# Feed-forward products of layers 0 to 2 by rows of tokens, five of their sixteen units by Strassen's scheme, and a written ScalarE order in stick-breaking attention

## The chip, the cores and the metric

One Trainium2 chip, one core, one launch. The metric is the device time of the program in microseconds (us). Engines are called as in the profile: PE (TensorE, matrix products), PEld (its weight loads), DVE (VectorE), ACT (ScalarE), POOL (GpSimd), SP (SyncE, which issues most DMAs).

## What is computed

A trunk of four layers over 256 tokens of 1024 features, all in float32. Layer i has a mixer (0 and 3 retention, 1 convolution, 2 stick-breaking attention), then a squared-ReLU feed-forward part:

```python
for i in range(DEPTH):                       # DEPTH = 4
    h = rms_norm(x, norm_mix[i])
    x = x + mixer_i(h)                       # retention, conv, stick-breaking, retention
    x = x + squared_relu_mlp(rms_norm(x, norm_ffn[i]), ffn_w1[i], ffn_w2[i])
return rms_norm(x, final_norm)

def squared_relu_mlp(xn, w1, w2):            # w1 1024 x 4096, w2 4096 x 1024
    h = jax.nn.relu(xn @ w1)
    return (h * h) @ w2
```

The stick-breaking mixer takes logits z of queries and keys, masks them, forms log-sigmoids and their running sums along the keys, exponentiates, and multiplies with the values; 16 heads of 64.

## The kernel before

**Number format.** Each float32 operand is cut in two: a rounded part hi (a cast on ACT) and the rest lo (a subtraction on DVE), and a product is hi·hi + hi·lo + lo·hi. For weights these are `wh` (L361, ACT, 128x1024) and `wl` (L368, DVE, 128x1024), written into five buffers each (pool `wp`), one pair for each unit of 128x1024 weights. Weights come as `raw` tiles of two units by DMA from SP.

**Layout.** x is kept with features on the partitions: four tiles of 128x512 (p = 0 to 3, each two blocks of 128 features by 256 tokens). The next mixer or feed-forward part takes `z`, eight tiles (z0 to z7, two for each x tile): hi by ACT (L475), lo by DVE (L476). `norm_sq` squares x (L486, ACT) and adds up over the tiles on POOL (L491); the sum over features then is a matmul with a column of constants (L436).

**The feed-forward part** (`ffn`, from L640). The first product makes 16 pairs of blocks of h (units p = 0 to 15, `pair_w`): each step is one matmul of 256 columns (lo of the weight, L558) and one of 512 (hi of the weight with hi and lo of z side by side, L562). `sum_w` adds the two halves (L605 ACT, L606 DVE), then ReLU, square, and the split into hi and lo (L411, L412): 32 tiles h of the pool `big`, two for each unit. In layers 0 to 2 the second product goes the same way with h in the place of z: four pairs (p = 0 to 3) over eight units of 512 rows, the weight as stationary operand. Where the last pair would leave the next mixer waiting, it is made of three matmuls of 256 columns a step (L542 to L544): all of p = 3 in layer 0, the last two of its eight units in layers 1 and 2. The squared norm factor, spread over the partitions (`norm_rb`), is multiplied in at the end (L704), the result is added to x (L705), and `norm_pair` makes z for the next mixer.

**Layer 3 already works another way** (`final`, L708): tokens are on the output's partitions. Four accumulators C[t, c] (t = token half, c = half of the 1024 output features) begin with 16 transposes of x. The h blocks are stationary, the weights (512 columns) move. Eleven of the sixteen units of 256 rows are plain: 24 matmuls each. Five (`FAST` = 0, 1, 13, 14, 15) go by Strassen's scheme: seven block products instead of eight, 21 matmuls; `fast_unit` forms their weight combinations (four additions L384, five casts L391 and five subtractions L392 of 128x512, beside one L361 and one L368), and `ffn` the h combinations (L661 to L670). `MIXED` is the order in which plain and Strassen units alternate, `REST` the four plain units at the end, first for c = 0, then for c = 1. All matmuls of it have line L722.

**What sets the order.** PE, DVE, ACT, POOL and SP each run their own queue in order. Most of it is arranged by a scheduler at build time. In the convolution PE and DVE (in its second half ACT and POOL too) follow the program text; in the stick-breaking mixer PE does, by a string of steps (`SB_ORDER`): p = projection of a unit, n = norms of q and k of one block of four heads, u and t = transposes of q and k, l = logits and masks, s = the ACT and DVE chain abs, exp, ln, max, split (L1549 to L1555), w = running sums and exp (L1568), v = values, m = product with the values. PSUM has eight banks: four `acc`, four `mis`.

**POOL in layer 0.** The convolution's 18 strips (L1045, a product of 128x512) are formed ahead of the convolution, in buffers of the pool `big` (36 buffers, handed on in turn). A strip can be written when the former tenant of its buffer has been used for the last time.

Of the kernel before, what the change touches and what calls it, by code (L numbers as in the profile page):

```python
# [15 lines left out]
P = 128  # L16
# [17 lines left out]
    "p00 p01 r p02 p03 p10 n0 p11 p12 p13 u0 t0 p20 n1 l0 s0 p21 p22 w02 p23 n2 w00 u1 t1 p30 l1 p31 p32 s1"  # L34
    " w01 w12 p33 w10 u2 t2 w11 v00 n3 l2 s2 v01 v02 w22 v03 u3 t3 w20 v10 l3 v11 s3 w21 v12 w32 v13 w31 w30"
    " m0 m1",
    "m2 m3",
)

# [18 lines left out]
FAST = (0, 1, 13, 14, 15)  # L58
MIXED = (2, 0, 3, 4, 1, 5, 13, 6, 14, 7, 15, 8)
# [8 lines left out]
def _plan():  # L68
    u = []
    for i in range(DEPTH):  # L70
# [30 lines left out]
        if i + 1 < DEPTH:  # L101
            for p in range(4):
                u += _b_pair("ffn_w2", i, p * 256, 8)
        else:
            u += [("ffn_w2", i, "a", kb, c * 512) for kb in MIXED for c in range(2)]
            u += [("ffn_w2", i, "a", kb, c * 512) for c in range(2) for kb in REST]
# [139 lines left out]
class Trunk:  # L246
    def __init__(self, ctx, tc, xT, w, prm, cst, fin, gn, out):
# [16 lines left out]
        self.un = 0  # L264
        nc = self.nc
# [217 lines left out]
    def norm_sq(self, p):  # L483
        nc = self.nc
        q = self.tmp()
        nc.scalar.activation(out=q, in_=self.x[p], func=AF.Square)  # L486
        if self.sq is None:
            self.sq = q
        else:
            a = self.tmp()  # L490
            (nc.vector if p == 3 and self.quick else nc.gpsimd).tensor_add(a, self.sq, q)  # L491
            self.sq = a
# [18 lines left out]
    def norm_rb(self):  # L511
        nc = self.nc
        sq = self.sq[:, :S]
        nc.gpsimd.tensor_add(sq, sq, self.sq[:, S:])
        hl = self.split(sq)
        ps = self.mis()
        for e in range(2):
            nc.tensor.matmul(ps[:, :S], self.cr["m1"], hl[:, e * S : (e + 1) * S], start=e == 0, stop=e == 1)
        b = self.bc.tile([P, S], F32, name=self.nm("rb"), tag="rb")
        nc.vector.tensor_scalar(out=b, in0=ps[:, :S], scalar1=-1.0 / D, scalar2=EPS, op0=ALU.mult, op1=ALU.add)  # L520
        nc.vector.reciprocal(out=b, in_=b)
        return b

    def zs(self, k):
        return self.z[k]
# [55 lines left out]
    def pair_x(self, name, l, c0, acts, nkb, x, rb):  # L581
        nc = self.nc
        ps, pe = [self.acc(), self.acc()], self.mis()

        def onto(a):
            t = self.tmp()
            nc.vector.tensor_mul(v3(t, 2, S), v3(a, 2, S), self.b2(rb))
            nc.vector.tensor_add(x, x, t)

        for kb in range(nkb):  # L590
            w = self.unit((name, l, "b", kb, c0))
            if kb < nkb - 2:
                self.mm_w(ps, w, acts, kb * 4, kb == 0, kb == nkb - 3, keep=True)
            else:
                if kb == nkb - 2:
                    onto(self.sum_w(ps))
                self.mm_b(pe, w, acts, kb * 4, kb == nkb - 2, kb == nkb - 1)
        onto(pe)

# [27 lines left out]
    def res_pairs(self, name, l, acts, nkb, group, evac, before=None):  # L627
        for g in range(4 // group):
            ps = [self.acc() for _ in range(group)]
            for kb in range(nkb):  # L630
                if before is not None:
                    before(kb)
                for p in range(group):
                    w = self.unit((name, l, "b", kb, (g * group + p) * 256))
                    self.mm_b(ps[p], w, acts, kb * 4, kb == 0, kb == nkb - 1)
                    if kb == nkb - 1:
                        evac(g * group + p, ps[p])


    def ffn(self, i, nxt):  # L640
# [4 lines left out]
        def act(ps):  # L645
# [27 lines left out]

        def factor(k):
            if k == (2 if last else 0):
                rb.append(self.bcast(self.r, "rb", keep=True) if last else self.norm_rb())
                for x in held:
                    act(x)

        held = []  # L680
        for p in range(16):
            ps = self.pair_w(
                "ffn_w1", i, p * 256, self.zs, keep=p >= (3 if last else 4),
                before=factor if p == (3 if last else 2) else None,
# [5 lines left out]
            if last and p == 0:  # L690
                with self.tc.high_priority():
                    self.norm_r(False)

        acts = lambda k: h[k]
        if last:
            self.final(i, h, fast)
            return
        self.norm_begin()
        for p in range(4):
            pw = ("ffn_w2", i, p * 256, acts, 8)  # L700
            if p < 3 or i == 0:
                ps = self.pair_w(*pw, keep=True) if p < 3 else self.pair_b(*pw)
                t = self.tmp()
                nc.vector.tensor_mul(v3(t, 2, S), v3(ps, 2, S), self.b2(rb[0]))  # L704
                nc.vector.tensor_add(self.x[p], self.x[p], t)  # L705
            else:
                self.pair_x(*pw, self.x[p], rb[0])
            self.norm_pair(p, *nxt)  # L708


    def final(self, i, h, fast):
        nc = self.nc
        kw = dict(skip_group_check=True)
        self.table("sqrt_and_others")
# [950 lines left out]
```

## Time and profile before

| what | value |
|---|---|
| median of three runs | 1337.06 us (1336.6 to 1338.1) |
| the profiled execution's own time | 1338.49 us |
| its span, first to last instruction | 1336.7 us |
| second product of layer 3, 16 transposes included (L722) | 1244.7 to 1330.5 us |
| DVE, ACT, POOL busy | 1012.0, 806.8, 134.3 us |
| DMA | 244.56 MB, mean 183 GB/s |

The time outside the span is 1.8 us. How to read the views: a row of a group gives the line, engine, operation, tiles (out<-in, buffer numbers left out), shape and count, then busy time and mean of one. A timeline row gives start, duration and what it is; in square brackets the idle time of the engine before it and what ended it. Matmuls overlap: the time that one takes on PE is the step from its start to the next one's start, less than its own duration.

### The profile page before, as it was taken

How to read it: one execution, taken by the hardware profiler on the slowest of the kernel's cores; microseconds unless marked ns; L12 is line 12 of the kernel's file. 1: busy time of each engine (PE TensorE's matmuls, PEld its weight loads, DVE VectorE, ACT ScalarE, POOL GpSimd, SP SyncE). 2: the span in 40 equal slices, each digit the busy share in tenths (PEclk: the TensorE clock that was granted, in tenths of full speed). 3: DMA queues.
4: the chain of work that ended last, by engine and by line, in shares of the span. 5: the costliest groups of instructions: out<-in, count | busy, mean ns of one | idle time of the engine just before them, and what ended most of it. 6: DMA issues, size and time to landing. Idle time of an engine off the chain costs nothing.

```text
span 1336.7 us, 20778 instructions
## 1 busy us (share of the span) xinstructions
PE 1326.3 (99%) x8174; PEld 1160.2 (87%) x8174; DVE 1012.0 (76%) x1689; ACT 806.8 (60%) x1275; POOL 134.3 (10%) x123
## 2 busy tenths in 40 slices
PE   9999999999999999999999999999999999999998
PEld 8988888888999898888878898888888888888886
DVE  7977768875688688765688588755698776798985
ACT  7555556764456477744568677744565555577663
POOL 3200002000269110000100010000110000100000
PEclk9999999999999999999999999999999999999999
DMA  8545555555445645555453345555554554555552
GB/s 311 211 172 186 179 190 185 192 193 187 184 163 147 217 171 200 192 190 191 174 186 126 126 162 189 190 190 191 185 187 173 190 184 152 213 187 182 187 189 95
DMA packets 41731, 244.56 MB, mean 183 GB/s; under 512 B 4512, under 2 KB 9248, under 8 KB 14240
## 3 DMA queue, kind: packets, MB, share of 16 engines
q1 hardware_dynamic: 40768, 240.60, 50.4%
q10 hardware_dynamic: 864, 2.62, 0.6%
q8 instruction: 64, 1.05, 0.3%
q14 instruction: 35, 0.29, 0.1%
HBM read 241.27 MB, written 1.93 MB: 182 GB/s over the span
## 4 chain that ended last, share of the span: by engine, by line
PE 95%; POOL 1%; ACT 1%; DVE 1%; issue 1%; DMA 0%; POOLq 0%; DVEq 0%; ACTq 0%
PE acc L562 33%; PE acc L558 17%; PE acc L1024 6%; PE acc L1026 6%; PE acc L1025 6%; PE acc L722 5%; PE acc L542 3%; PE acc L544 3%; PE acc L543 3%; PE mis L562 2%; PE mis L558 1%; PE acc L1326 1%; POOL big L1122 1%; PE mis L722 1%; PE acc L1193 1%
## 5 line engine op out<-in xcount | busy, mean ns | idle before, releaser
L368 DVE TENSOR_TENSOR wl<-raw,wh 128x1024 fp32r<-128x1024 f32 (+1 forms) x435 | 539.4, 1245 | 206.5 <-ACT wh L361 200.8
L361 ACT CAST wh<-raw 128x1024 fp32r<-128x1024 f32 (+1 forms) x435 | 451.1, 1042 | 311.8 <-PE acc L562 153.5
L562 PE MATMUL acc<-z,wh 128*128 128x512 f32 x1152 | 399.4, 394 | 0.0
L558 PE MATMUL acc<-z,wl 128*128 128x256 f32 x1152 | 317.1, 280 | 0.9 <-DVE t L606 0.9
L562 PE MATMUL acc<-big,wh 128*128 128x512 f32 x800 | 277.5, 393 | 0.0
L562 PEld LDWEIGHTS acc<-z,wh 128*128 128x128 f32 x1152 | 214.3, 187 | 47.0
L558 PE MATMUL acc<-big,wl 128*128 128x256 f32 x800 | 221.4, 279 | 0.0
L558 PEld LDWEIGHTS acc<-z,wl 128*128 128x128 f32 x1152 | 216.5, 189 | 3.6 <-PE acc L562 1.1
L562 PEld LDWEIGHTS acc<-big,wh 128*128 128x128 f32 x800 | 149.4, 187 | 33.5
L558 PEld LDWEIGHTS acc<-big,wl 128*128 128x128 f32 x800 | 150.3, 189 | 0.7
L1024 PE MATMUL acc<-wh,z 128*128 128x512 f32 x352 | 137.9, 392 | 0.0
L1026 PE MATMUL acc<-wh,z 128*128 128x512 f32 x352 | 137.2, 390 | 0.0
L1025 PE MATMUL acc<-wl,z 128*128 128x512 f32 x352 | 137.2, 390 | 0.0
L491 POOL TENSOR_TENSOR t<-t,t 128x512 f32<-128x512 f32 x23 | 35.7, 1553 | 884.1 <-ACT t L486 814.6
L605 ACT COPY t<-acc 128x256 f32<-128x256 f32 x176 | 61.2, 371 | 100.2 <-PE acc L562 98.6
L606 DVE TENSOR_TENSOR t<-acc,t 128x256 f32<-128x256 f32 x176 | 68.3, 420 | 39.4 <-ACT t L605 39.0
L1026 PEld LDWEIGHTS acc<-wh,z 128*128 128x128 f32 x352 | 66.1, 188 | 14.7 <-issue 0.8
L1024 PEld LDWEIGHTS acc<-wh,z 128*128 128x128 f32 x352 | 66.1, 188 | 14.0 <-issue 0.8
L1025 PEld LDWEIGHTS acc<-wl,z 128*128 128x128 f32 x352 | 66.1, 188 | 13.2
L722 PE MATMUL acc<-wh,big 128*128 128x512 f32 x200 | 63.7, 390 | 0.0
L542 PE MATMUL acc<-z,wh 128*128 128x256 f32 x224 | 63.6, 284 | 0.0
L544 PE MATMUL acc<-z,wl 128*128 128x256 f32 x224 | 63.4, 283 | 0.0
(306 smaller groups left out, 1907.4 us busy)
## 6 DMA issues: line engine op xcount, KB each, us to landing
raw<-in_w SPq DMA_DIRECT2D x214, 1024.0 KB, 4.8
big<-in_gn SPq DMA_DIRECT2D x16, 256.0 KB, 5.3
raw<-in_w SPq DMA_DIRECT2D x7, 512.0 KB, 7.5
raw<-hd SPq DMA_DIRECT2D x8, 263.0 KB, 4.7
raw<-hd SPq DMA_DIRECT2D x8, 131.5 KB, 3.9
wh<-in_w ACTq DMA_DIRECT2D x2, 512.0 KB, 7.0
wl<-in_w ACTq DMA_DIRECT2D x2, 512.0 KB, 8.8
hd<-big SPq DMA_DIRECT2D x6, 143.5 KB, 2.1
```

The lines of the kernel that those rows point to most:

```text
L361: nc.scalar.copy(hi[:, s], src[:, s])
L368: self.nc.vector.tensor_sub(lo[:, s], src[:, s], hi[:, s])
L542: nc.tensor.matmul(o, wh[:, kk, cs], ah, start=st, stop=False, **kw)
L544: nc.tensor.matmul(o, wl[:, kk, cs], ah, start=False, stop=en, **kw)
L558: mm = nc.tensor.matmul(ps[m][:, :S], wl[:, kk, cs], a[:, :S], start=first and kk == 0, stop=False, **kw)
L562: nc.tensor.matmul(ps[m], wh[:, kk, cs], a, start=False, stop=last and kk == 3, **kw)
L605: nc.scalar.copy(o[:, s], ps[m][:, S:])
L606: nc.vector.tensor_add(o[:, s], ps[m][:, :S], o[:, s])
L722: self.tc.keep_in_program_order(nc.tensor.matmul(o, l, r, **k, **kw))
L1024: nc.tensor.matmul(ps[t], zh[:, s], wh[:, kk], start=k == 0, stop=False, skip_group_check=True)
L1025: nc.tensor.matmul(ps[t], zh[:, s], wl[:, kk], start=False, stop=False, skip_group_check=True)
L1026: nc.tensor.matmul(ps[t], zl[:, s], wh[:, kk], start=False, stop=k == 7, skip_group_check=True)
```

## The change

1. Layers 0 to 2 take the second product by rows of tokens as layer 3 does; the shared code is `down`, the two users are `middle` (layers 0 to 2) and `final`. `middle` starts C from zero, scales each C[t, c] by the token's factor while evacuating it (`scaled`, ACT; the last one half on ACT, half on DVE), transposes the result back (`turn`: 16 transposes a layer) and adds it to x from PSUM (`onto`). C[0, 0] and C[1, 0] are evacuated while the four last units of c = 1 run; C[0, 1] while the last twelve matmuls of C[1, 1] run; C[1, 1] after the last matmul. Its transposes, additions and z4 to z7 are a closure `rest` that the next mixer calls when it asks for z2.
2. `FAST` becomes (5, 6, 13, 14, 15) and `MIXED` (0, 5, 1, 2, 6, 3, 13, 4, 14, 7, 15, 8), for all layers. The split of h is done by DVE for p < 4 and by ACT for the others, in all layers (before: DVE in layers 0 to 2, ACT in layer 3).
3. The factor of layers 0 to 2 is a column for each token half (`norm_sums`, `norm_r2`) instead of a row over the partitions (`norm_rb`).
4. Stick-breaking: the masks are the first matmuls of a block's logits instead of the last; `s` is cut into its three parts, values are evacuated in a step `c` of their own; the unit's casts are called three units ahead (`SB_AHEAD`); ACT follows the program text, as PE did already.
5. Convolution: the fourth unit is fetched one step later, and the norm's column sums come in the third unit instead of the second.

The core of the diff:

```diff
 SB_ORDER = (
-    "p00 p01 r p02 p03 p10 n0 p11 p12 p13 u0 t0 p20 n1 l0 s0 p21 p22 w02 p23 n2 w00 u1 t1 p30 l1 p31 p32 s1"
+    "p00 p01 p02 r p03 p10 n0 p11 p12 p13 u0 t0 n1 p20 l0 s02 p21 s00 p22 s01 w02 p23 w00 u1 t1 n2 p30 l1 s12 p31 s10"
...
+SB_AHEAD = 3
-FAST = (0, 1, 13, 14, 15)
-MIXED = (2, 0, 3, 4, 1, 5, 13, 6, 14, 7, 15, 8)
+FAST = (5, 6, 13, 14, 15)
+MIXED = (0, 5, 1, 2, 6, 3, 13, 4, 14, 7, 15, 8)
...
+    def norm_r2(self, sums):
+        nc = self.nc
         ps = self.mis()
+        for t in range(2):
+            self.tc.keep_in_program_order(self.colsum(ps[:, t : t + 1], sums[:, t * P : (t + 1) * P], self.sc(1024)))
+        r2 = self.col(2, "r2")
+        nc.vector.tensor_scalar(out=r2, in0=ps[:, :2], scalar1=EPS, scalar2=None, op0=ALU.add)
+        nc.vector.reciprocal(out=r2, in_=r2)
+        return r2
 
     def zs(self, k):
+        if self.rest and k == 2:
+            rest, self.rest = self.rest, None
+            rest()
         return self.z[k]
...
-            how = "act" if last else "dve"
+            how = "dve" if p < 4 else "act"
             h.extend((self.split(s[:, :S], how), self.split(s[:, S:], how)))
-            if last and p in FAST:
+            if p in FAST:
...
+    def middle(self, i, h, fast, sums, nxt):
+        nc = self.nc
+        r2 = self.norm_r2(sums)
+        y, pt = {}, {}
+
+        def scaled(C, t, c, *cuts):
+            y[t, c] = self.tmp()
+            for s, on in cuts or ((slice(0, 512), "act"),):
+                if on == "act":
+                    nc.scalar.activation(out=y[t, c][:, s], in_=C[t, c][:, s], func=AF.Copy, scale=r2[:, t : t + 1])
+                else:
+                    nc.vector.tensor_scalar(
+                        out=y[t, c][:, s], in0=C[t, c][:, s], scalar1=r2[:, t : t + 1], scalar2=None, op0=ALU.mult
+                    )
+
+        def turn(t, c):
+            for q in range(4):
+                p = 2 * c + q // 2
+                if p not in pt:
+                    pt[p] = self.mis()
+                o = (q % 2) * S + t * P
+                self.tc.keep_in_program_order(
+                    nc.tensor.transpose(pt[p][:, o : o + P], y[t, c][:, q * P : (q + 1) * P], self.id)
+                )
...
+        def hook(C, at):
+            if at == 0:
+                for t in range(2):
+                    scaled(C, t, 0)
+                self.norm_begin()
+            if at == (REST[1], 0, 0):
+                for t in range(2):
+                    turn(t, 0)
+                for p in range(2):
+                    onto(p)
+                    self.norm_pair(p, *nxt)
+            if at == (REST[-2], 0, 1):
+                scaled(C, 0, 1)
+            if at == (REST[-1], 0, 1):
+                turn(0, 1)
+                for p in (2, 3):
+                    onto(p, 0)
+
+        C = self.down(i, h, fast, None, hook)
+        scaled(C, 1, 1, (slice(0, S), "act"), (slice(S, 512), "dve"))
+
+        def rest():
+            turn(1, 1)
+            for p in (2, 3):
+                onto(p, 1)
+                self.norm_pair(p, *nxt, False)
+            for p in (2, 3):
+                self.norm_sq(p, nc.vector)
+
+        self.rest = rest
...
-        with self.tc.manual_schedule(engines={mybir.EngineType.PE}):
+        with self.tc.manual_schedule(engines={mybir.EngineType.PE, mybir.EngineType.Activation}):
             go(SB_ORDER[0])
```

Two places of the build's order follow, and a third on POOL; in them the numbers tell buffers apart, and what stands in brackets is what an instruction waits for. First PE at the end of layer 0's second product. Before, its last rows (L542 to L544 on `big`) are followed by the convolution's first (on `z`):

```order
L542 MATMUL acc_3690<-big_3125,wh_3895 128x256
L543 MATMUL acc_3690<-big_3125,wh_3895 128x256
L544 MATMUL acc_3690<-big_3125,wl_3896 128x256
L542 MATMUL acc_4007<-z_3306,wh_3989 128x256 [waits Activation_49]
L543 MATMUL acc_4007<-z_3306,wh_3989 128x256
L544 MATMUL acc_4007<-z_3306,wl_3990 128x256 [waits DVE_49]
```

The same place of the change; `acc_3191` is C[1, 1], `t_790_3863` its scaled copy, `mis` the bank of the transposes:

```order
L678 MATMUL acc_3191<-wl_3832,big_2956 128x512
L678 MATMUL acc_3191<-wh_3831,big_2956 128x512
L764 MATMUL mis_3849<-cst,t_790_3863 128x128 [waits DVE_49,Activation_49]
L764 MATMUL mis_3849<-cst,t_790_3863 128x128
L764 MATMUL mis_3852<-cst,t_790_3863 128x128 [waits DVE_49]
L764 MATMUL mis_3852<-cst,t_790_3863 128x128
L545 MATMUL acc_3933<-z_3797,wh_3919 128x256
L546 MATMUL acc_3933<-z_3797,wh_3919 128x256
```

The transposes of C[1, 1] now stand directly behind its last matmul, since the scheduler put the convolution's steps on z0 and z1 ahead of the last six matmuls of C[1, 1]; it does the same before the stick-breaking mixer, while before the retention of layer 3 eight matmuls on z0 to z3 stand between.

Second, ACT in the stick-breaking mixer, from the last part of the first block's chain (L1549 to L1551) on, before; L1476 squares the next block's projections, L1568 is the exp that frees a bank of the first block's logits (`mis_7395`), L1503 copies transposed q:

```order
L361 CAST wh_7664<-raw_7600 128x1024 [waits PE_49]
L1551 ACTIVATE t_1341_7435<-t_1340_7434 128x512 [waits DVE_49,Activation_49]
L1476 ACTIVATE t_1354_7500<-acc_7348 128x512 [waits DVE_49,PE_49]
L1476 ACTIVATE t_1356_7505<-acc_7349 128x512 [waits PE_49]
L361 CAST wh_7714<-raw_7712 128x1024 [waits DMAHW4_49]
L1568 ACTIVATE big_7481<-mis_7395 128x512
L1568 ACTIVATE big_7530<-mis_7396 128x512 [waits PE_49]
L1503 ACTIVATE big_7537<-mis_7532,prm 128x512 [waits PE_49]
```

The same place of the change, where L1589 to L1591 are the chain, L1608 the exp and L1545 the copy:

```order
L359 CAST wh_7415<-raw_7385 128x1024
L1589 ACTIVATE t_1473_7431<-mis_7361 128x512 [waits PE_49]
L1590 ACTIVATE t_1474_7432<-t_1473_7431 128x512 [waits Activation_49]
L1591 ACTIVATE t_1475_7433<-t_1474_7432 128x512 [waits DVE_49,Activation_49]
L1608 ACTIVATE big_7445<-mis_7359 128x512 [waits PE_49]
L359 CAST wh_7449<-raw_7447 128x1024 [waits DMAHW3_49]
L1608 ACTIVATE big_7469<-mis_7360 128x512 [waits PE_49]
L1545 ACTIVATE big_7476<-mis_7471,prm 128x512 [waits PE_49]
```

The exp that frees the bank stands directly behind the chain; the squares of the next block have moved behind the transposes.

Third, POOL in layer 0. Before, strips (L1045) and the sum of squares (L491) alternate:

```order
L1045 TENSOR_TENSOR big_3945<-cst,prm 128x512 [waits PE_49]
L491 TENSOR_TENSOR t_681_3500<-t_653_3312,t_680_3498 128x512 [waits DVE_49,Activation_49,Pool_49]
L1045 TENSOR_TENSOR big_3947<-cst,prm 128x512 [waits PE_49]
L1045 TENSOR_TENSOR big_3949<-cst,prm 128x512 [waits PE_49]
L1045 TENSOR_TENSOR big_3951<-cst,prm 128x512 [waits PE_49]
```

In the change (strips L1078, sum L489):

```order
L1078 TENSOR_TENSOR big_3901<-cst,prm 128x512 [waits PE_49]
L1078 TENSOR_TENSOR big_3903<-cst,prm 128x512 [waits PE_49]
L1115 MEMSET big_4108 128x31 [waits DVE_49,PE_49]
L1115 MEMSET big_4111 128x31 [waits DVE_49,PE_49]
L489 TENSOR_TENSOR t_781_3805<-t_777_3794,t_780_3803 128x512 [waits DVE_49,Activation_49]
```

All 18 strips now stand ahead of the only sum of squares left on POOL. In the build, each waits for the last matmul on an h tile or a Strassen tile that had its buffer: the 18, in turn, for tiles of the units 1, 1, 2, 2, 6, 6, 6, 6, 3, 3, 13, 13, 4, 4, 14, 14, 7, 7 of the second product.

More of the change, by code (lines that the diff above doesn't have):

```diff
@@ L689, in ffn @@
                 act(ps)
[L690 to L694, printed above, removed]
+            if p == 0:
+                if last:
+                    with self.tc.high_priority():
+                        self.norm_r(False)
+                else:
+                    sums = self.norm_sums()
         if last:
             self.final(i, h, fast)
[L697 to L708, printed above, removed]
```

251 lines of the change are left out of this document (121 added, 130 removed).

## Prediction, made before the run

> **What bounds the kernel now.** I read the page first, then the chain that ended last, then single stretches of PE's timeline.
>
> ```profile
> span 1336.7 us, 20778 instructions
> PE 1326.3 (99%) x8174; PEld 1160.2 (87%) x8174; DVE 1012.0 (76%) x1689; ACT 806.8 (60%) x1275; POOL 134.3 (10%) x123
> PEclk9999999999999999999999999999999999999999
> PE 95%; POOL 1%; ACT 1%; DVE 1%; issue 1%; DMA 0%; POOLq 0%; DVEq 0%; ACTq 0%
> ```
>
> PE is busy in 99% of the span, holds 95% of the chain, and its granted clock is full in every slice. So a change is worth what it takes from or adds to PE's sequence of matmuls, and other engines count only where PE stands still. I take the price of a matmul from steps between starts in stretches without a gap: 174 steps of the old second product, 48 of its three-matmul form, 111 of layer 3's product. First and last start of each (the first stretch counts L558, the second L542, the third L722):
>
> ```profile
> 880.01 0.28 PE L558 MATMUL acc<-big,wl 128*128 128x256 f32 x1
> 939.99 0.28 PE L558 MATMUL acc<-big,wl 128*128 128x256 f32 x1
> ...
> 363.02 0.28 PE L542 MATMUL acc<-big,wh 128*128 128x256 f32 x1
> 379.94 0.28 PE L542 MATMUL acc<-big,wh 128*128 128x256 f32 x1
> ...
> 1304.95 0.61 PE L722 MATMUL acc<-wh,big 128*128 128x512 f32 x2
> 1329.88 0.39 PE L722 MATMUL acc<-wl,big 128*128 128x512 f32 x1
> ...
> 122.51 0.87 PE mis L976 x8
> ```
>
> A 256+512 step takes 59.98/173 = 0.3467 us, a 3x256 step 16.92/47 = 0.360, a 512 matmul 24.93/110 = 0.2266, and a 128x128 transpose 0.87/8 = 0.109.
>
> **Part 1: PE's own work.** Out go 192 + 240 + 240 = 672 steps of 0.3467 (233.0 us) and 64 + 16 + 16 = 96 steps of 0.360 (34.6). In come, for each of three layers, 11 x 24 + 5 x 21 = 369 matmuls of 0.2266 (250.9 in all) and 16 transposes of 0.109 (5.2). The small matmuls for the norm factor (two of 256 columns out, two column sums in) cancel. Sum: 267.6 - 256.1 = 11.5 us less. All of it is on the path, since PE is.
>
> **Part 2: can DVE feed it?** Layer 3 runs this very scheme, and shows it. These are the whole of it and four cycles of one Strassen and one plain unit (45 matmuls, 10.2 us):
>
> ```profile
> 1244.60:1330.50 85.90, 85.90 (x388) 70.98 (x386) 67.72 (x98) 46.88 (x66) 0.00 (x0) 1.00 0.42 153
> 1257.40:1267.60 10.20, 10.20 (x47) 8.45 (x46) 9.95 (x14) 4.26 (x7) 0.00 (x0) 1.00 0.79 265
> 1267.60:1277.80 10.20, 10.20 (x47) 8.45 (x46) 9.01 (x13) 5.97 (x8) 0.00 (x0) 1.00 0.57 214
> 1277.80:1288.00 10.20, 10.20 (x47) 8.45 (x46) 8.95 (x13) 5.97 (x8) 0.00 (x0) 1.00 0.58 208
> 1288.00:1298.20 10.20, 10.20 (x47) 8.45 (x46) 8.46 (x11) 5.96 (x8) 0.00 (x0) 1.00 0.56 214
> ```
>
> The columns are stretch, length, then busy PE, PEld, DVE, ACT, POOL. PE never stands still, but DVE is busy for 8.5 to 9.95 of 10.2 us: it has 1.2 us to spare in a cycle. In layers 1 and 2 nothing else needs DVE there, and it even starts lighter, since ReLU goes through ACT in those layers and through DVE only in layer 3 (0.689 us for each of the last three units, row below). I cost layers 1 and 2 at nothing. ACT has over 4 us to spare in a cycle. DMA moved 208 to 265 GB/s without holding PE.
>
> Layer 0 differs: POOL makes the 18 strips there. What a strip does to DVE shows in the old layer 0, in rows of DVE and POOL:
>
> ```profile
> 358.66 1.23 DVE L368 TENSOR_TENSOR wl<-raw,wh 128x1024 fp32r<-128x1024 f32 x1 [1.55 <-ACT wh L361]
> 361.21 1.50 DVE L704 TENSOR_TENSOR t<-t,rb 128x512 f32<-128x512 f32 x1
> 362.63 2.07 DVE L368 TENSOR_TENSOR wl<-raw,wh 128x1024 fp32r<-128x1024 f32 x1
> ...
> 229.13 1.09 POOL L1045 TENSOR_TENSOR big<-cst,prm 128x512 f32<-128x512 f32 x1 [12.38 <-PE mis L518]
> 361.11 10.35 POOL L1045 TENSOR_TENSOR big<-cst,prm 128x512 f32<-128x512 f32 x7 [16.31 <-PE acc L544]
> ...
> L648 DVE SCALAR_TENSOR_TENSOR t<-t,rb 128x512 f32<-128x512 f32 x16 | 11.0, 689 | 0.3
> ```
>
> From 361.1 on, strips and DVE alternate, and a DVE subtraction takes 2.07 instead of 1.23 us: 0.84 more for each strip. Before, that fell into a stretch where DVE waited 1.5 us between instructions. Now the 18 strips are released one by one through the Strassen stretch. How far DVE is ahead there, layer 3 shows at its second Strassen unit, by the unit's last weight half on DVE and its first matmul:
>
> ```profile
> 1267.17 0.68 DVE L392 TENSOR_TENSOR wl<-t,wh 128x512 fp32r<-128x512 f32 x1
> ...
> 1267.94 0.68 PE mis L722 x3
> ```
>
> That half was ready at 1267.85 and used 18 matmuls after 1267.94, at 1272.0: 4.2 us ahead. In layer 0: 4.2, plus 3 x 0.69 = 2.1 without L648, less four strips (3.4) before that point: 2.9. Then the cycle of units 6 and 3 meets six strips (5.0 against 1.2 to spare, -3.8), that of 13 and 4 four (3.4 against 1.25, -2.1), that of 14 and 7 four (3.4 against 1.7, -1.7): PE waits 0.9 + 2.1 + 1.7 = 4.7. Some strips will fall into DVE's own short waits, so I take 4.0. The ends are 0 (the lead and those waits cover it) and 18 x 0.84 = 15.1 (nothing does).
>
> The Trainium skill bears on this: "SBUF — State Buffer", section "SBUF: two separate sides", says that the port pair shared by DVE and GpSimd is an exclusive lock, held for a whole instruction, between a GpSimd operation and a DVE operation with two SBUF inputs. The trace agrees in kind, with 0.84 us where a strip alone takes 1.09; by the whole instruction the upper end would be 18 x 1.09 = 19.6.
>
> **Part 3: the hand-overs.** Before, PE passes to the next mixer without a gap, behind steps that hide the last additions to x. Now the transposes of C[1, 1] wait for its evacuation, and before the convolution and the stick-breaking mixer nothing stands between. The nearest rows are the kernel's own end (last matmul to ACT), a 256-column evacuation, and the makers of z:
>
> ```profile
> 1330.11 0.39 PE L722 MATMUL acc<-wh,big 128*128 128x512 f32 x1
> 1330.54 0.60 ACT L805 ACTIVATE t<-acc 128x512 f32<-128x512 f32 x1 [0.30 <-PE acc L722]
> ...
> L605 ACT COPY t<-acc 128x256 f32<-128x256 f32 x176 | 61.2, 371 | 100.2 <-PE acc L562 98.6
> L606 DVE TENSOR_TENSOR t<-acc,t 128x256 f32<-128x256 f32 x176 | 68.3, 420 | 39.4 <-ACT t L605 39.0
> L475 ACT ACTIVATE z<-head 128x256 fp32r<-128x256 f32 x16 | 7.4, 503 | 2.9 <-DMA head<-in_x 2.9
> L476 DVE SCALAR_TENSOR_TENSOR z<-head,z 128x256 fp32r<-128x256 f32 x16 | 7.1, 478 | 5.9 <-ACT z L475 5.9
> ```
>
> From the slot's end (1330.11 + 0.23) to ACT's start are 0.2 us, the half takes 0.37, and I estimate 0.1 back to PE: 0.67 for each of two places. In the convolution z4 and z5 then come just in time (the transposes 0.44, the addition 0.42, ACT 0.50, DVE 0.48, together 1.84, against 0.44 and twelve matmuls of 0.12 on z2 and z3), z6 some 0.4 late, since x3's addition stands behind z4 and z5 on DVE. The stick-breaking mixer has 2.7 us of matmuls there, the retention eight steps ahead and eight behind. Sum 0.67 x 2 + 0.45 = 1.8; ends 0.7 and 4 (each link 0.2 us slower in three layers).
>
> **Part 4: waits that go.** In the stick-breaking mixer the second transposes of a block waited once for a bank, whose exp stood on ACT behind squares and a cast:
>
> ```profile
> 698.28 0.60 PE L1498 MATMUL mis<-cst,t 128*128 128x128 f32 x4
> 699.88 0.66 PE L1498 MATMUL mis<-cst,t 128*128 128x128 f32 x4 [0.99 <-ACT big L1568]
> ...
> 697.79 0.60 ACT t L1476
> 698.39 0.93 ACT wh L361
> 699.32 0.51 ACT big L1568
> ```
>
> 698.28 + 4 x 0.109 to 699.88 is 1.2 us. The new order puts that exp ahead of the squares: -1.2. Moving the masks alone changes no count; I give it nothing. The other wait is layer 3's first product, where DVE (L670, a Strassen combination of unit 0) held an evacuation:
>
> ```profile
> 1181.37 0.39 PE L562 MATMUL acc<-z,wh 128*128 128x512 f32 x1
> 1182.62 0.36 PE L558 MATMUL acc<-z,wl 128*128 128x256 f32 x1 [0.86 <-DVE t L606]
> ```
>
> 1181.37 + 0.23 to 1182.62 is 1.0 us. Units 0 and 1 leave `FAST`, but DVE takes over those units' casts: -0.9. The later column sums in the convolution I cost at nothing: they still stand ahead of the fourth unit, whose 2.9 us hide the factor; if that cover goes, what is late next is POOL's chain of taps, by a few tenths.
>
> **The sum.** -11.5 + 4.0 + 1.8 - 1.2 - 0.9 = -7.8 us, from 1338.49 to 1330.7 for a profiled execution; that one stands 1.4 above the median of the runs, so the median goes from 1337.06 to 1329.3.
>
> **Rivals.** (a) The strips cost nothing: -11.8 in all, 1325.3. For it speaks that PE has no gap at all in layer 3 and that a strip may fall into a DVE wait; against it that DVE is busy 9.95 of 10.2 us in the first cycle. (b) The fixed ACT order brings back waits. Between u and the next block's exp, ACT's queue holds instructions that wait for PE, and the next casts stand behind them. One wait for a bank in each of the four blocks (4 x 1.2), and the old one not saved: +6.0 on the forecast, 1335.3. Against it: casts are three units ahead, 3 x 12 x 0.2266 = 8.2 us. (c) Slower: all strips land on the path. DVE is then short by 15.1 in layer 0, and -11.5 + 15.1 + 1.8 - 1.2 - 0.9 = +3.3 gives 1340.4. It decides from a wait of 11.8 us in layer 0 on. For it: Strassen units already fill DVE. Against it: DVE's lead and 1.2 us to spare in each of three cycles, some 7 us. By the skill's whole-instruction lock (same page and section) it would be 7.8 slower, 1344.9; the 0.84 of the trace speaks against that.
>
> **How the numbers follow.** A measurement of this kernel tells 0.2% (2.7 us) from no change: faster means under 1334.4, slower over 1339.7. Chances: forecast 0.60, (a) 0.22, (b) 0.11, (c) 0.07. Of (b) a third lies under 1334.4. That gives faster 0.85, same 0.08, slower 0.07. The range leaves out (c) and the worse part of (b): from 1324.0 (rival (a) with hand-overs at 0.7) to 1335.5.
>
> **What would show it.** Right: second products of layers 1 and 2 at 85.5 us (369 x 0.2266 + 16 x 0.109 + waits under 0.3), layer 0's at 89 to 90, with DVE subtractions of about 2 us and PE waiting for `wl` in units 13, 14, 15; a PE gap of 0.6 to 0.7 ahead of the last transposes in layers 0 and 1; no gap at the second block's transposes in stick-breaking. Wrong: PE waits for `wh` or `wl` in layers 1 and 2, over 8 us of waits in layer 0, or PE waits for ACT inside the stick-breaking mixer.

## The result, and the profile after

The changed kernel took 1344.51 us (median of 4 runs, 1344.31 to 1344.88), the kernel before 1337.03 on the same chip: ratio 1.0055, 95% interval 1.0038 to 1.0072. That is slower by 7.5 us, where 1329.3 was forecast. The profiled execution of the changed kernel took 1344.88 us with a span of 1343.1, against 1338.49 and 1336.7.

First the busy times of the changed kernel, then its table of what PE waited for (total, times, longest):

```profile
PE 1323.0 (99%) x7703; PEld 1135.1 (85%) x7703; DVE 1070.8 (80%) x1802; ACT 861.3 (64%) x1407; POOL 136.7 (10%) x118
...
PE acc L678 <- DVE wl L366: 6.4, 7, 3.4
PE acc L1228 <- issue: 2.4, 2, 1.3
...
PE mis L764 <- ACT t L751: 1.1, 2, 0.6
PE acc L545 <- ACT z L473: 0.6, 2, 0.4
PE acc L565 <- DVE z L474: 0.5, 1, 0.5
PE mis L678 <- DVE wl L390: 0.5, 1, 0.5
PE mis L441 <- DVE ry L429: 0.5, 1, 0.5
```

Of the same table of the kernel before, the longest row and the one for "issue":

```profile
PE mis L301 <- POOL t L273: 1.3, 1, 1.3
...
PE acc L1193 <- issue: 0.4, 1, 0.4
```

Both pages say "PE 99%". What tells is the list of waits: before, no row of it was over 1.3 us (this one is there after the change too), now PE waits for weight halves (`wl`), scaled copies (`t`), `z` and the norm factor (`ry`). The list adds up to some 13 us, and doesn't say what was lost net of the saving; for that the stages are compared. This table takes the first matmul of each stage in the two traces (lengths in us; the forecast is the prediction's own sum for that stage):

| stage, by first matmuls | before | after | measured | forecast |
|---|---|---|---|---|
| layer 0's second product to the convolution's first strip matmul | 137.08 | 146.86 | +9.8 | +0.9 |
| convolution from there to layer 1's first product | 51.25 | 52.90 | +1.65 | 0 |
| layer 1's first product | 89.15 | 90.51 | +1.4 | 0 |
| layer 1's second product, stick-breaking, to layer 2's first product | 206.99 | 204.40 | -2.6 | -4.1 |
| layer 2's first product | 89.13 | 89.24 | +0.1 | 0 |
| layer 2's second product to the retention's values | 134.15 | 132.73 | -1.4 | -3.6 |
| from there to the last matmul | 328.77 | 326.24 | -2.5 | -0.9 |
| sum | | | +6.4 | -7.7 |

**Layer 0, POOL against DVE.** Timelines of DVE and of POOL in layer 0's second product (start, length, line; a row can hold several):

```profile
316.72 1.53 DVE L390 TENSOR_TENSOR wl<-t,wh 128x512 fp32r<-128x512 f32 x1
318.18 1.54 DVE L382 TENSOR_TENSOR t<-t,raw 128x512 f32<-128x512 f32 x1
319.64 2.07 DVE L366 TENSOR_TENSOR wl<-raw,wh 128x1024 fp32r<-128x1024 f32 x1
321.64 1.54 DVE L382 TENSOR_TENSOR t<-t,raw 128x512 f32<-128x512 f32 x1
...
308.82 17.27 POOL L1078 TENSOR_TENSOR big<-cst,prm 128x512 f32<-128x512 f32 x8 [96.20 <-PE acc L678]
```

From start to start, a half of 512 columns takes DVE 1.46 us and one of 1024 columns 2.00. Eight strips took POOL 17.27 us: the first waited for DVE, then one strip went between every two DVE instructions. PE came to a stop for the missing halves, the longest time here:

```profile
333.32 0.61 PE L678 MATMUL acc<-wh,big 128*128 128x512 f32 x2
337.33 0.50 PE L678 MATMUL acc<-wl,big 128*128 128x512 f32 x1 [3.40 <-DVE wl L366]
...
338.72 1.06 PE L678 MATMUL acc<-wh,big 128*128 128x512 f32 x2
339.57 0.63 PE L678 MATMUL acc<-wl,big 128*128 128x512 f32 x1
...
337.30:341.30 4.00, 3.96 (x11) 3.14 (x12) 4.00 (x6) 0.00 (x0) 0.00 (x0) 0.58 0.44 133
341.30:345.00 3.70, 3.70 (x18) 3.03 (x17) 2.26 (x4) 1.11 (x2) 1.50 (x2) 0.99 1.00 396
```

Behind the wait of 3.40 us the next matmuls are 0.425 us apart (two steps from 338.72 to 339.57) instead of 0.2266. The two rows by stretches below show why: the granted clock (the number behind the five engines) is 0.58 for 4 us, then 0.99. Eight matmuls at 0.2 us more are 1.6 us on top of the wait. The Trainium skill, "TensorE: Matmul & The Clock Gate", Part 1, gives such a rule: half clock after an idle window of about 3.4 us, full clock after as long a busy one. The trace agrees here, though in three other runs the half clock came behind shorter waits (2.79, 2.76 and 1.69 us, below), and there the measurement decides. The prediction had not used the rule.

**The hand-over to the convolution**, PE's timeline:

```profile
390.10 0.40 PE L678 MATMUL acc<-wh,big 128*128 128x512 f32 x1
391.06 0.96 PE L764 MATMUL mis<-cst,t 128*128 128x128 f32 x4 [0.56 <-ACT t L751]
391.78 0.36 PE L545 MATMUL acc<-z,wh 128*128 128x256 f32 x1
...
393.83 0.39 PE L545 MATMUL acc<-z,wh 128*128 128x256 f32 x1 [0.38 <-ACT z L473]
...
396.10 0.38 PE L545 MATMUL acc<-z,wh 128*128 128x256 f32 x1 [0.18 <-ACT z L473]
...
402.42 0.68 PE L441 MATMUL mis<-cst,ry 128*128 128x128 f32 x4 [0.47 <-DVE ry L429]
```

The forecast had the first wait (390.10 + 0.23 to 391.06: 0.73) and a late z. In the trace z4 is late, z6 is late, and the norm factor is late too.

**The convolution itself**, whose instructions are the old ones, has two new stalls in its strip matmuls (L1228). PE's timeline, and the row of the DMA queue that loads code:

```profile
454.80 1.41 PE L1228 MATMUL acc<-raw,big 128*32 128x128 f32 x38
457.25 0.55 PE L1228 MATMUL acc<-raw,big 128*32 128x128 f32 x10 [1.04 <-issue]
...
461.84 1.65 PE L1228 MATMUL acc<-raw,big 128*32 128x128 f32 x44
464.82 0.32 PE L1228 MATMUL acc<-raw,big 128*32 128x128 f32 x2 [1.33 <-issue]
...
q8 instruction: 60, 0.98, 0.3%
```

"issue" means that PE waited for nothing that the profile shows; q8 is the queue that the page calls "instruction". More on it below.

### The profile page after: what moved, and what is told of

It is laid out like the page before. It is cut to its first block, busy times and chain, and to the rows that moved or that the text cites. A ratio compares the mean times of both kernels' runs of the same rounds, so it can differ in the third digit from the quotient of the medians.

```text
span 1343.1 us, 20137 instructions
## 1 busy us (share of the span) xinstructions
PE 1323.0 (99%) x7703; PEld 1135.1 (85%) x7703; DVE 1070.8 (80%) x1802; ACT 861.3 (64%) x1407; POOL 136.7 (10%) x118
## 4 chain that ended last, share of the span: by engine, by line
PE 67%; DVE 2%; ACT 1%; issue 0%; ACTq 0%; DVEq 0%
PE acc L565 16%; PE acc L678 14%; PE acc L561 8%; PE acc L1057 4%; PE acc L1059 4%; PE acc L1058 4%; PE mis L678 3%; PE acc L545 2%; PE acc L546 2%; PE acc L547 2%; PE acc L1228 1%; PE acc L1361 1%; PE mis L565 1%; PE mis L561 1%; DVE wl L366 1%; PE mis L1602 0%
## 5 line engine op out<-in xcount | busy, mean ns | idle before, releaser
L366 DVE TENSOR_TENSOR wl<-raw,wh 128x1024 fp32r<-128x1024 f32 (+1 forms) x420 | 517.1, 1241 | 132.8 <-ACT wh L359 131.1
L359 ACT CAST wh<-raw 128x1024 fp32r<-128x1024 f32 (+1 forms) x420 | 434.1, 1041 | 240.4 <-PE acc L678 75.3
L561 PE MATMUL acc<-z,wl 128*128 128x256 f32 x1152 | 316.2, 280 | 0.1
L678 PE MATMUL acc<-wh,big 128*128 128x512 f32 x800 | 257.0, 392 | 0.0
L678 PEld LDWEIGHTS acc<-wh,big 128*128 128x128 f32 x800 | 151.0, 189 | 31.0
L678 PE MATMUL acc<-wl,big 128*128 128x512 f32 x400 | 157.4, 394 | 6.4 <-DVE wl L366 6.4
L489 POOL TENSOR_TENSOR t<-t,t 128x512 f32<-128x512 f32 x18 | 29.0, 1610 | 805.7 <-ACT t L484 642.0
L678 PEld LDWEIGHTS acc<-wl,big 128*128 128x128 f32 x400 | 75.5, 189 | 25.1 <-DVE wl L366 9.3
L590 DVE TENSOR_TENSOR t<-acc,t 128x256 f32<-128x256 f32 x154 | 59.5, 419 | 19.5 <-ACT t L589 17.7
L389 ACT CAST wh<-t 128x512 fp32r<-128x512 f32 x80 | 47.1, 619 | 42.9 <-PE acc L678 18.1
L545 PE MATMUL acc<-z,wh 128*128 128x256 f32 x224 | 63.9, 285 | 0.6 <-ACT z L473 0.6
L546 PE MATMUL acc<-z,wh 128*128 128x256 f32 x224 | 63.6, 284 | 0.3
```

The source lines that it names most:

```text
L359: nc.scalar.copy(hi[:, s], src[:, s])
L366: self.nc.vector.tensor_sub(lo[:, s], src[:, s], hi[:, s])
L545: nc.tensor.matmul(o, wh[:, kk, cs], ah, start=st, stop=False, **kw)
L546: nc.tensor.matmul(o, wh[:, kk, cs], al, start=False, stop=False, **kw)
L561: mm = nc.tensor.matmul(ps[m][:, :S], wl[:, kk, cs], a[:, :S], start=first and kk == 0, stop=False, **kw)
L590: nc.vector.tensor_add(o[:, s], ps[m][:, :S], o[:, s])
```

## The experiments

Each run is compared with the kernel before on the same chip; "us" is the difference of the medians. The changed kernel stands at +7.5. Theory A: strips on POOL make DVE late in layer 0. Theory B: Strassen's work alone overloads DVE there. Theory C: the hand-overs lack cover.

### Strips only set to zero (theory A against B)

```
-                nc.gpsimd.tensor_mul(v3(o, 16, 32), ..., ...)
+                nc.gpsimd.memset(o, 0.0)
```

> The 18 strips are only set to zero, in the same buffers and at the same places on POOL (left out: the products that fill them, so the taps that the convolution takes from them are zero). Theory A (a strip on POOL and a two-operand instruction on DVE hold each other up, DVE falls behind, PE waits for weight halves and then runs 3.4 us at half clock): DVE's subtractions of layer 0 are back at 0.60 and 1.14 us a step, PE's waits of 7.6 us and the 1.6 us at half clock go, layer 0's second product takes about 89 instead of 98.2 us, and the time is about 1335.3. Theory B (Strassen's own work on DVE is too much in layer 0, strips or not): at least 5 us of the waits stay, 1342 to 1344.5.

Ratio 0.9968 (0.9956 to 0.9981), 1333.67 us: -4.4, 11.9 better than the changed kernel. Layer 0's second product by stretches (length, busy PE, PEld, DVE, ACT, POOL, clock), of this run and of the changed kernel; then DVE and PE of this run around its second Strassen unit:

```profile
293.74:382.31 88.57, 87.75 (x399) 72.11 (x399) 72.06 (x100) 52.57 (x72) 11.60 (x27) 1.00 0.55 190
...
315.35 0.69 DVE L390 TENSOR_TENSOR wl<-t,wh 128x512 fp32r<-128x512 f32 x1
315.95 0.69 DVE L382 TENSOR_TENSOR t<-t,raw 128x512 f32<-128x512 f32 x1
316.83 1.23 DVE L366 TENSOR_TENSOR wl<-raw,wh 128x1024 fp32r<-128x1024 f32 x1 [0.20 <-ACT wh L359]
317.97 0.68 DVE L382 TENSOR_TENSOR t<-t,raw 128x512 f32<-128x512 f32 x1
...
319.81 0.39 PE L678 MATMUL acc<-wl,big 128*128 128x512 f32 x1
```

```profile
293.60:391.80 98.20, 91.06 (x400) 72.83 (x399) 86.43 (x100) 52.66 (x72) 33.16 (x27) 0.98 0.49 172
```

DVE needs 72.06 instead of 86.43 us for the same hundred instructions, is back at 0.60 and 1.14 us a step, and PE is through 9.6 us earlier. Theory A holds, B falls: Strassen alone leaves one wait of 0.34 us, behind the first Strassen unit. (Of the other 2.3, 1.5 are the convolution's second stall, absent in this run's profile.) The rows also give the lead that the prediction estimated: the unit's last half is ready at 316.04 (315.35 + 0.69) and used at 319.81, 3.8 us.

### Strips behind the Strassen units

```
+        late = self.bigt()
+        u0, u1, u2 = (late[:, f * n : (f + 1) * n] for f in range(3))
+        for u in (u0, u1, u2):
+            nc.gpsimd.tensor_copy(u[:, :1], self.e1[:, :1])
...
+        v0, v1, v2 = u0, u1, u2
```

> The same strips, computed in full, but held on POOL until the first evacuation behind the last Strassen unit of layer 0. Theory A: the waits of layer 0 go as with strips that are only set, 1335.5, up to 1337 if strips now meet the evacuations or come late for the convolution. Theory B: no gain in layer 0, 1342 to 1345.

Ratio 0.9988 (0.9979 to 0.9998), 1336.22 us: -1.8. The waits in the Strassen stretch are gone with the strips complete, which confirms A. Part comes back behind it, where strips now meet the evacuations: PE's longest new wait in layer 0 is that of the first transposes.

```profile
371.81 1.25 PE L765 MATMUL mis<-cst,t 128*128 128x128 f32 x8 [1.03 <-ACT t L752]
```

### Twelve strips of eighteen (is the price linear?)

```
+                if v is v0:
+                    nc.gpsimd.memset(o, 0.0)
+                else:
                     nc.gpsimd.tensor_mul(...)
```

> Of the 18 strips the first of every three is only set to zero (left out: its products, and so a third of the taps that the convolution takes from strips). By theory A with its ledger (18 strips cost DVE 15.5 us, of which 7.5 are covered by its lead and spare time, the other 8 become waits, and 1.6 go at half clock): 12 strips cost 10.3, 2.8 are left as waits, none long enough for the half clock, and the time is 0.7 us above before. Rival (each strip costs PE its share, 9.6/18 us, covered or not): 4.2 us above before.

Ratio 1.0016 (1.0007 to 1.0025): +1.9, between the two expectations. PE's longest wait for a half, the clock behind it, and this run's longest stall in the convolution:

```profile
333.70 0.50 PE L678 MATMUL acc<-wl,big 128*128 128x512 f32 x1 [2.59 <-DVE wl L366]
...
333.70:338.00 4.30, 4.30 (x19) 3.57 (x20) 4.30 (x6) 0.62 (x1) 0.09 (x1) 1.00 0.47 160
...
461.34 0.31 PE L1231 MATMUL acc<-raw,big 128*32 128x128 f32 x2 [2.76 <-issue]
```

Up to the convolution it is 5.1 us behind the run without strips (142.34 against 137.26). Twelve strips cost DVE 10.3 us at 0.86, so 5.2 were covered, where 7.5 of the 15.5 of all eighteen were; the cover is no fixed amount. The half clock did not come behind 2.59 us, as expected. It did come behind the stall of 2.76 us: from 461.5 to 465.0 the granted clock is 0.52. (The profiled execution took 1342.93 us, the median is 1339.63.)

### Strips from one-operand products

```
+                for c in range(16):
+                    nc.gpsimd.tensor_scalar(
+                        out=o[:, c * 32 : (c + 1) * 32], in0=self.c("id32", 32), scalar1=v[:, i * 16 + c : i * 16 + c + 1],
+                        scalar2=None, op0=ALU.mult,
+                    )
```

> Each strip is computed as 16 products of the 128x32 identity with a scalar per partition, in place of one product of two 128x512 operands; same buffers, place and result (one sum of squares of layer 0 goes from POOL to DVE so that it doesn't part the strips). If only a POOL instruction with two operands holds DVE up: DVE is back at 0.60 and 1.14 us a step, 4 us faster than the kernel before, as with strips that are only set. If any POOL instruction that reads does: DVE is held up as long as POOL is busy, 18 strips of 1.6 us or more, and the time is 7 us or more above before.

Ratio 1.0361 (1.0347 to 1.0375): +48.5. The time is that of the second expectation, but not for its reason. POOL's first four products, the group of all 288, and PE's longest wait:

```profile
308.90 8.14 POOL L1080 TENSOR_SCALAR big<-cst,prm 128x32 f32<-128x32 f32 x4 [96.21 <-PE acc L678]
...
L1080 POOL TENSOR_SCALAR big<-cst,prm 128x32 f32<-128x32 f32 x288 | 144.9, 531 | 96.2 <-PE acc L678 96.2
...
PE acc L547 <- DVE wl L366: 47.7, 1, 47.7
...
DVE mis L1146 <- POOL big L1117: 54.4, 1, 54.4
...
293.70:380.00 86.30, 86.13 (x391) 71.29 (x392) 71.54 (x99) 51.31 (x70) 71.10 (x88) 1.00 0.54 195
```

In layer 0, the last row, DVE is not held up at all: 71.54 us busy, with POOL busy beside it for 71.10. Now POOL gives way: its first four products of 128x32 took 8.14 us, against 0.36 each where DVE was idle. These products have one operand and are also smaller, so the run doesn't tell which of the two decides. So the strips end only after 145 us of POOL. The memset of the convolution's tiles (L1117) stands behind them, DVE's first tap waits for that, and a weight half behind the tap on DVE's written-out order keeps PE waiting for 47.7 us.

### Layer 0 as before

```
+        if i == 0:
...
+                pw = ("ffn_w2", i, p * 256, lambda k: h[k], 8)
+                ps = self.pair_w(*pw, keep=True) if p < 3 else self.pair_b(*pw)
+                t = self.tmp()
+                nc.vector.tensor_mul(v3(t, 2, S), v3(ps, 2, S), self.b2(rb[0]))
+                nc.vector.tensor_add(self.x[p], self.x[p], t)
...
-        if last:
+        elif last:
```

> Layer 0's second product as before the change (matmuls of 256 and 512 columns, no Strassen, no transposes); layers 1 to 3 and the stick-breaking mixer as changed. If the loss lies in layer 0 and its hand-over to the convolution: the 9.8 us that the changed kernel is behind at the convolution's first matmul go, 1334.7, and 1332.8 if the two stalls of 1.3 and 1.6 us inside the convolution go too. Rival (layers 1 and 2 lose as much by the new product): above 1340.

Ratio 0.9975 (0.9964 to 0.9985), 1334.10 us: -4.0. As expected, the loss sits in layer 0 and what follows it; layers 1 to 3 gain.

### The hand-overs (theory C)

Two runs. The first keeps matmuls on z0 and z1 behind C[1, 1] and takes the weight units on z0 to z3 first; the second does that and takes the norm factor one unit later (the last two lines).

```
-        pw1 = [(c + p * 256, kb) for p in range(4) for c in (D, 0) for kb in range(2)]
+        pw1 = [(c, kb) for kb in range(2) for c in (D, 0)]
+        pw1 += [(c + p * 256, kb) for p in range(1, 4) for c in (D, 0) for kb in range(2)]
...
+    def pinned(self, m):
+        return self.tc.keep_in_program_order(m) if self.rest else m
...
-                    (lambda kk: self.norm_r(False) if kk == 1 else None) if n == 2 else None,
+                    (lambda kk: self.norm_r(False) if kk == 1 else None) if n == 3 else None,
```

> The next mixer's first matmuls on z0 (stick-breaking) or z0 and z1 (convolution) are kept between the last matmul of C[1, 1] and its transposes, and the convolution's first two weight units on z0 to z3 come ahead of the two on z4 to z7. Theory C (the hand-over costs because nothing covers the evacuation ahead of the transposes and the chain to z4): the 1.0 us ahead of the transposes in layers 0 and 1 and 1.7 us of waits for z4 to z6 in the convolution go, 1340.8. Rival (the waits only move to the next step in the chain, the norm factor or z6): 1 us or less, 1343.5 to 1344.5.

Ratio 1.0034 (1.0021 to 1.0047): +4.4. Of the 3 us better than the changed kernel, the convolution's hand-over has none: that stage took 146.88 us against 146.86. All waits for `t` and `z` went there, and this one came, in the next link of the chain (the column sums wait for the squares' sum on DVE), with a stretch at half clock behind it, the last row:

```profile
395.83 0.28 PE L553 MATMUL acc<-z,wl 128*128 128x256 f32 x1
397.80 1.02 PE L437 MATMUL mis<-cst,t 128*128 128x1 f32 x8 [1.69 <-DVE t L492]
...
400.20:403.60 3.40, 3.34 (x17) 3.08 (x16) 2.67 (x10) 1.42 (x2) 0.00 (x0) 0.50 0.73 289
```

In that stretch matmuls of 256 columns step at 0.21 us instead of 0.12. The wait is only 1.69 us, but the eight matmuls behind it have one column each. The gain is 1.1 us in the stick-breaking mixer (its wait ahead of the transposes is gone) and 1.5 in the convolution, where one of the two "issue" stalls fell away. So the rival was right for the convolution. With the factor later:

> The run with moved first matmuls, and the convolution's norm factor (column sums, square root, broadcast) one weight unit, 2.9 us, later. Theory C (the chain from C[1, 1] to the norm factor needs cover, and got too little): the 1.9 us ahead of the column sums go, with 0.4 ahead of the broadcast, 1.5 to 2.2 us faster than the run with moved first matmuls, 2.4 to 3.1 us above before. Rival (DVE, with taps and gates queued, takes the gain back): as that run, 4.6 us above before.

Ratio 1.0027 (1.0017 to 1.0036): +3.4. The stage drops from 146.88 to 144.22 us, 2.7 better, and the column sums no longer wait:

```profile
399.19 0.28 PE L553 MATMUL acc<-z,wl 128*128 128x256 f32 x1
399.31 0.95 PE L437 MATMUL mis<-cst,t 128*128 128x1 f32 x8
```

With the 1.69 us the half clock behind them went too. Of the 2.7, 1.2 us are lost again in the strip matmuls, where PE now waits for POOL too. Theory C holds once the whole chain is covered, from the last matmul to the factor.

### The stick-breaking part, taken out and alone

```
-    "p00 p01 p02 r p03 p10 n0 p11 p12 p13 u0 t0 n1 p20 l0 s02 p21 s00 p22 s01 w02 p23 w00 u1 t1 n2 p30 l1 s12 p31 s10"
...
+    "p00 p01 r p02 p03 p10 n0 p11 p12 p13 u0 t0 p20 n1 l0 s0 p21 p22 w02 p23 n2 w00 u1 t1 p30 l1 p31 p32 s1"
...
-        with self.tc.manual_schedule(engines={mybir.EngineType.PE, mybir.EngineType.Activation}):
+        with self.tc.manual_schedule(engines={mybir.EngineType.PE}):
```

> The stick-breaking mixer alone as before the change (masks last, only PE's order written out); all else as changed (7.5 us slower than the kernel before). If the new order only saves the bank wait of 1.2 us and costs nothing else: this is 0.5 to 1.2 us slower than the changed kernel, 8.0 to 8.7 us above before. Rival (the fixed ACT order costs waits elsewhere in the mixer): faster than the changed kernel, 5 to 7 us above before.

Ratio 1.0093 (1.0079 to 1.0106): +12.3, so 4.8 slower than the changed kernel: both expectations missed. PE's timeline behind the hand-over, and the stretch that follows:

```profile
675.99 0.39 PE L1058 MATMUL acc<-wh,z 128*128 128x512 f32 x1
679.17 1.49 PE L433 MATMUL mis<-cst,t 128*128 128x1 f32 x8 [2.79 <-DVE t L488]
...
683.00:687.00 4.00, 4.00 (x12) 3.10 (x12) 0.00 (x0) 0.93 (x1) 0.00 (x0) 0.58 0.00 0
```

The old order takes the column sums (step r) one unit earlier, and with the new second product their input is late: 2.79 us, then half clock again. The bank wait of 1.0 us is back as well. So by this trace the new order's later r is a part of the hand-over; alone it was not run. On the kernel before:

> The kernel before with the changed stick-breaking mixer alone (masks first, ACT's order written out). The step of the prediction (the bank wait of 1.2 us goes, nothing else changes): 1.2 us faster than before. Rival (ACT's fixed order brings waits back, as the prediction's second rival had it): no change or slower by up to 5 us; then a wait of PE for ACT stands in the mixer.

Ratio 0.9994 (0.9985 to 1.0003): -0.7, not told apart from no change by the medians. In its profile the bank wait is gone, no wait for ACT stands in the mixer, and from its first projection to layer 2's first product it takes 117.14 us instead of 118.04. So -0.9 by the trace, where -1.2 was forecast.

### Two versions put together

> Strips held until behind the Strassen units, the hand-overs of the run with moved first matmuls, and the convolution's norm factor one weight unit later. If the three losses are separate, they add up: -9.0 (strips) -2.1 (hand-over as measured) -1.5 (the wait for the norm factor) against the changed kernel, which makes it 5 us faster than the kernel before, about 1333 where before is 1338. Rival (strips behind the Strassen units and the hand-over fight for the same stretch of DVE and POOL): no faster than the late strips alone, 1.6 us under before.

This is the late strips with both hand-over edits. Ratio 0.9978 (0.9968 to 0.9987): -3.3, short of the 5 expected. The convolution's first strip matmul comes 1.2 us earlier than with late strips alone, and then waits for its data:

```profile
443.93 1.14 PE L1244 MATMUL acc<-raw,big 128*32 128x128 f32 x32 [1.95 <-DMA raw<-hd]
```

Last, layer 0 as before, with layers 1 to 3 changed, the hand-over to stick-breaking covered, and the first Strassen unit one place later:

```
-MIXED = (0, 5, 1, 2, 6, 3, 13, 4, 14, 7, 15, 8)
+MIXED = (0, 1, 5, 2, 6, 3, 13, 4, 14, 7, 15, 8)
```

> Layer 0's second product as before the change (as in the run with the old layer 0: 3.3 us under before); layers 1 and 2 by rows of tokens, with their first Strassen unit one place later and the stick-breaking mixer's first matmuls on z0 between the last matmul of C[1, 1] and its transposes. If what the two layers lose is the 0.34 us wait for the first Strassen unit's successor in each and the 1.0 us hand-over of layer 1: 5 us faster than before. If these only move, 3.3 as with the old layer 0.

Ratio 0.9957 (0.9944 to 0.9969), 1332.28 us: -5.5, faster than both kernels. PE's timeline at the hand-over to stick-breaking: the matmuls on z0 (L1090 to L1092) hide the scaled copy.

```profile
658.18 0.40 PE L710 MATMUL acc<-wh,big 128*128 128x512 f32 x1
658.41 0.39 PE L1090 MATMUL acc<-wh,z 128*128 128x512 f32 x1
...
659.78 0.60 PE L796 MATMUL mis<-cst,t 128*128 128x128 f32 x4
```

## Why the prediction was wrong

**Part 1, PE's work: right.** The matmuls are as many as counted, and the step of the new product measures 0.2267 us in gapless stretches of layers 0 to 2. So the 11.5 us were taken out.

**Part 2, layers 1 and 2: nearly right.** DVE feeds the scheme there. Only behind the first Strassen unit does PE wait, 0.34 us in each layer. The run with that unit one place later has no such wait.

**Part 2, strips in layer 0: the step that failed first.** The price was right: 0.84 us forecast, 0.86 measured, 14.4 in all on DVE where 15.1 was the upper end. What failed is "4.2, plus 3 x 0.69 = 2.1 without L648" for DVE's lead: without strips it is 3.8. The 2.1 did not come: in layers 0 to 2 ReLU and square follow each other on ACT, and in that run DVE stands still for 1.36 us at the start of the stage, until ACT's square (L625) is done. The strips also did not come one by one: eight of them took POOL from 308.82 to 326.09 without a break, before DVE's spare time of later cycles could serve. The gaps between PE's starts came to 7.5 us (6.9 of them are the rows of waits for `wl`; 0.3 stand there without strips too), where 4.7 was worked out and 4.0 taken. And a wait was priced at its own length, while the longest cost 1.6 us more by the half clock. In all 9.6 us (146.86 less 137.26) stand against the 4.0 of the sum. Rival (c) named the right place and sign, but got its 3.3 us from two errors: strips at 15.1, which is too much, and the rest as in the forecast, which is too little. That its second figure, 1344.9 with strips at 19.6 us, lies 0.4 from the result is luck of the same kind.

**Part 3, hand-overs: 1.8 forecast, about 7 measured.** Without strips, layer 0's stage is at 137.26 us; 137.08 less the 4.2 of PE's saving would be 132.9. So 4.4 are lost, 0.3 of them the Strassen wait and 4.1 the hand-over. PE's steps beyond the gapless ones show 3.4 of it: 0.9 at the transposes (forecast 0.67), 1.0 at z4 (nothing), 0.8 at z6 (0.45) and 0.6 at the norm factor (nothing). Layer 1 has 0.9 at its transposes, and layer 2 loses some 1.9 (its stage gained 1.4 of 3.6, 0.3 of the loss being the Strassen wait). The step that failed is the sum "0.67 x 2 + 0.45", in two ways. The chain from the transposes to the second half of z4 took 3.3 us (391.06 to 394.35), where 1.84 was added up. And the sum stopped at z6: the squares of x2 and x3, their sum, the column sums and the factor hang on the same chain, and "The later column sums in the convolution I cost at nothing" named a cover of 2.9 us that the run with moved matmuls showed to be used up already (1.69 us of waiting there). Layer 2's hand-over was not taken apart.

**Part 4:** the stick-breaking term was -1.2 and measures -0.9. Layer 3's wait went, as forecast. The last stage gained 1.6 more than the 0.9, and layer 1's first product lost 1.4. Over most of one first product each, the step behind a 512-column matmul is 0.235 or 0.236 us (median) instead of 0.230 to 0.232: before in layer 3's, now in layer 1's. Why is open; the two nearly cancel.

**Not in the prediction:** 1.65 us in the convolution, whose instructions did not change. PE's "issue" row there went from 0.4 to 2.4 us; with strips only set, one of the two stalls is absent and the stretch takes 51.4 us, against 51.25 before.

Of the 14.1 us between the two sums of the table, then, the strips make 5.6, the hand-overs some 5, the three waits behind a first Strassen unit 1.0 and the convolution 1.65.

## What to carry to other kernels

When work moves from one engine to another under a full PE, price the wait of PE by the lead that the feeding engine really has at that point, read from its last write and PE's first use, and remember that a long wait can bring the slow clock behind it (here 1.6 us on top of 3.40). A transposed or scaled result is not handed over when its transposes are done: follow the chain to the last thing that the next stage needs from it, and count the cover for all of it. A helper's loop on a shared resource (here POOL's strips) belongs where the fed engine has slack, and a change need not pay in every layer: of the versions run, the fastest left layer 0 as it was, and the rest of the change, its hand-over mended, gained 5.5 us.

## What the runs showed of the hardware that was not expected

- **Two-operand POOL work and DVE.** POOL's 128x512 product alternates with DVE and adds 0.86 us to each DVE instruction; POOL's one-operand 128x32 product gives way to DVE without slowing it and takes up to 5.3 us instead of 0.36; a POOL memset of 128x512 does neither (0.53 us).
- **Half clock.** It came behind waits of 3.40, 2.79 and 2.76 us, and behind one of 1.69 us followed by eight one-column matmuls, and not behind 2.59. It lasted 3.4 us each time, and 6.8 behind the 2.79 us. So the length of one wait doesn't decide alone; what does was not tried.
- **Code.** Stalls of up to 2.8 us in strip matmuls, put down to "issue", stand in twelve of the thirteen kernels at the same places of PE's code and not of its work. Counted over all of PE's recorded instructions (matmuls, weight loads and semaphore instructions), the matmul behind such a stall is number 5826, 6082 or 6338, to within one, so in steps of 256, while the strip matmuls begin at number 4822, 4865 or 5240. Those stalls end 2.2 to 2.5 us after the start of a 16 KB transfer on q8 (2.8 to 3.3 at 5826 where layer 0 is the old one). The Trainium skill, "Runtime: NRT & Kernel Launch", "Instruction fetch mechanics", says that code is loaded in 16 KiB blocks of 256 instructions and that crossing a block is mostly hidden; in this stretch, with a matmul every 0.03 us, it is not. That loading code causes the stalls is inferred from these places and times. What decides how long one lasts was not tried: runs with the same count differ (one or two stalls, the second 0.3 to 2.8 us).
